# Feed-forward stage of an encoder trunk: joining copies ordered behind the last weight cast, and every weight unit cast in two pieces

## The chip, the cores and the metric

The kernel runs on one core of a Trainium2 chip. The metric is the device time of one execution in microseconds. TensorE (PE) does the matrix products and loads its weights beside them (PEld), VectorE (DVE), ScalarE (ACT) and GpSimd (POOL) do the rest, and SyncE (SP) issues the DMAs.

## The reference

Two layers of an encoder block on 256 tokens of width 1024, in float32. Each layer mixes a gated linear attention and a grouped-query attention, and is followed by a SwiGLU feed-forward stage of hidden width 2816, which is where the change acts, and by a per-layer embedding:

```python
gate, up = jnp.split(rms_norm(h, g_ffn_pre) @ w_ffn_in, 2, axis=-1)
h = h + rms_norm((jax.nn.silu(gate) * up) @ w_ffn_out, g_ffn_post)
e = p_i @ w_ple_proj
h = h + rms_norm(jax.nn.sigmoid(h @ w_ple_gate) * e, g_ple_post)
```

## The kernel before

**Products in three parts.** Every float32 operand of a product is split into a high part (a rounding to the format fp32r) and a low part, the remainder. A product is three matmuls: high by high, high by low, low by high (`mm3`, line 98). `split` (line 110) makes the parts: a cast on ScalarE (line 112) and a subtraction on VectorE (line 108).

**The stream of weights.** All weights come through `Stream` (line 210) in units of 128 x 2048, 1 MB each. A unit is loaded by SP into one of two buffers `raw` (line 259), is cast into a tile `wh` on ScalarE, and its remainder goes into `wl` on VectorE. The pools hold four `wh` and four `wl` tiles, so that a cast waits until TensorE has read the unit that held its slot. `take` hands the next unit to TensorE's code, `done` returns one, and `fill` then writes the casts of further units into the program, up to `depth` units ahead. `put` (line 265) cuts the unit into `parts` pieces, each with its own cast and subtraction: two halves of 128 x 1024, or the whole of 128 x 2048 while `ws.wide` is set.

**The feed-forward stage.** The hidden width is cut into 11 blocks of 256. The string `FFN` (line 38) gives the order in which the stage works through units: `u` is one of two units of a plain block (`block`, line 1268; 24 matmuls of 128x512), `1` to `7` are the seven steps of a pair of blocks (`pair`, `seven`; 12 matmuls each), `o` is a unit of the output matrix for both halves of the tokens (24 matmuls). The pair follows a scheme with seven products instead of eight, for which sums of weight units are made on VectorE (line 289). For these, two units are loaded into tiles lent from the `wh` and `wl` pools (in the profile `lent`), one into a tile `big`, and the fourth comes later as `raw`. Steps 3 to 5 and 7 of a pair add to the accumulator of an earlier step in place; before step 7 that accumulator must have been read by the subtraction that follows step 5 (`times(a, form(3), False, lambda: vsub(p5, p5, a))`, line 630).

**The transposes of the hidden values.** The gated values of a block lie with tokens on the partitions; the output product needs them transposed. `turn_words` (line 391) does this by DMA, with a generator in three stages: ScalarE copies the 16-bit words apart (line 401); SP issues the transposing DMA (line 407); ScalarE joins the words (line 413 for a plain block, line 419 for a half of a pair's), and `Split.put` casts the result and subtracts (tiles `big`, lines 112 and 108). Between the stages it yields a number of ticks, and a tick follows every few matmuls in the program's text. With `far` set, which is so for the feed-forward stage's blocks outside the last pair, the buffers of the last two stages are two halves of one tile `mid`.

**What sets the order.** A scheduler orders each engine's instructions by its own estimate of when they can run; each engine then works strictly in that order. `tc.issue_after(ins)` ties the instructions that a block traces on the engine of `ins` behind `ins`.

Of the kernel before, what the change touches and what calls it, by code (L numbers as in the profile page):

```python
# [18 lines left out]
P = 128  # L19
T = 256  # L20
# [30 lines left out]
def trunk_kernel(ctx: ExitStack, tc: tile.TileContext, a: dict, out: bass.AP):  # L51
# [7 lines left out]
    nc = tc.nc  # L59
# [13 lines left out]
    def nm(s):  # L73
        uid[0] += 1
        return f"{s}_{part[0]}_{uid[0]}"

    def big(dt=F32):
        return bigp.tile([P, 2048], dt, tag="big", name=nm("big"))

    def mid(dt=F32):  # L80
        return b4p.tile([P, 1024], dt, tag="mid", name=nm("mid"))
# [7 lines left out]
    def t512():  # L89
        return smp.tile([P, 512], F32, tag="t512", name=nm("t512"), bufs=7)  # L90
# [16 lines left out]
    def vsub(out, in0, in1):  # L107
        nc.vector.tensor_tensor(out=out, in0=in0, in1=in1, op=ALU.subtract)  # L108

    def split(hi, lo, src):  # L110

        nc.scalar.copy(hi, src)  # L112
        vsub(lo, src, hi.bitcast(F32))


    h = cp.tile([P, 2, D], F32, tag="h", name="h")
# [21 lines left out]
    def unit(w, kh, c0):  # L138

        return lambda t: [  # L140
            (
                t[:, :2048].rearrange("p (k c) -> p k c", c=512),
                w[kh * 512 : (kh + 1) * 512, c0 : c0 + 512].rearrange("(k p) c -> p k c", p=P),
            )
        ]
# [28 lines left out]
    for l in range(DEPTH):  # L174
# [12 lines left out]
        pairs = [[unit(w, kh, c + b * 256) for kh in range(2) for c in (0, HIDDEN)] for b in PAIRS]  # L187
# [9 lines left out]
    class Load:  # L197


        def __init__(self, make, own=None, waits=False):  # L200
            self.make, self.own, self.waits, self.raw, self.n = make, own, waits, None, 0
# [8 lines left out]
    class Stream:  # L210
# [7 lines left out]

        def __init__(self, depth):
            self.depth, self.held, self.room, self.ready, self.open = depth, 0, 0, [], False  # L220
            self.loads, self.jobs, self.lend, self.wide = [], [], False, False
            pairs = {}
            for item in plan:
                if callable(item):
                    x = Load(item)
                    self.loads.append(x)
                    self.jobs.append(lambda x=x: self.plain(x))
                else:
                    units, n = item
                    if n == 1:  # L230
                        b11, b12, b21, b22 = units
                        x, z = (Load(b, lambda tag=tag: self.lent(tag), tag == "wh") for b, tag in ((b11, "wh"), (b12, "wl")))
                        y, q = Load(b22, big), Load(b21)
                        pairs[id(units)] = x, y, z, q
                        self.loads += [x, y, z]
                    if n == 5:
                        self.loads.append(q)
                    self.jobs.append(lambda p=pairs[id(units)], n=n: self.step(n, *p))
# [23 lines left out]
                    between()  # L262
                x.n = sum(math.prod(dst.shape[1:]) for dst, _ in moves)

        def put(self, x, parts=None):

            wh = wp.tile([P, UNIT], F32R, tag="wh", name=nm("wh"))
            wl = wp.tile([P, UNIT], F32R, tag="wl", name=nm("wl"))
            self.ready.append((wh, wl))
            self.held += 1  # L270
            parts = parts or (1 if self.wide else 2)
            cuts = [slice(j * x.n // parts, (j + 1) * x.n // parts) for j in range(parts)]
            return [(wh[:, c], wl[:, c], x.raw[:, c]) for c in cuts]

# [6 lines left out]

        def made(self, x):
            for piece in self.put(x):
                split(*piece)

        def step(self, n, x, y, z, q):
            def add(to, other):
# [18 lines left out]
        def fill(self):  # L306
            while self.open and self.held < self.depth and self.jobs:
                pieces = self.jobs.pop(0)()
                for piece in pieces or ():
                    split(*piece)  # L310
                if pieces:
                    self.load()

# [9 lines left out]
    ws = Stream(4)  # L323
# [36 lines left out]
    class Split:  # L360
# [30 lines left out]
        def turn_words(self, src, k, n, hf=None, far=False):  # L391

            x = lambda: t512()[:, : n * P * (2 if hf is None else 1)]
            w = x()
            w16 = w.bitcast(U16)  # L400
            nc.scalar.copy(
                w16.rearrange("p (s c) -> p s c", s=2), src.bitcast(U16).rearrange("p (c s) -> p s c", s=2)
            )
            yield SENT
            r, z = [t[:, : n * P * (2 if hf is None else 1)] for t in halves(mid())] if far else (x(), None)
            r16 = r.bitcast(U16)
            nc.sync.dma_start_transpose(out=r16.rearrange("p (r t) -> p r t", t=P), in_=w16)
            yield LANDED
            z = x() if z is None else z
            z16 = z.bitcast(U16)  # L410
            if hf is None:
                for i in range(2):
                    nc.scalar.copy(
                        z16.rearrange("p (k h t s) -> p h s k t", k=2, h=2, s=2)[:, i],
                        r16.rearrange("p (s h k t) -> p h s k t", h=2, k=2, s=2)[:, i],
                    )
                self.put(z, k, n, 0, T)
            else:
                nc.scalar.copy(z16.rearrange("p (c s) -> p s c", s=2), r16.rearrange("p (s c) -> p s c", s=2))
                self.put(z, k, n, hf * P, P)  # L420

        def tok(self, k, hf):
            return [t[:, 0, :] for t in self.at(k, 1, hf * P, P)]
# [68 lines left out]
    def halves(t):  # L492
        return [t[:, j * 512 : (j + 1) * 512] for j in range(2)]
# [309 lines left out]
    for l in range(DEPTH):  # L803
# [219 lines left out]
        for x in range(2):  # L1023
            o = project_t(uT)
            for i in range(2):
                dst = qk[:, x, 2 * i : 2 * i + 2, :]
                src = o[i].rearrange("p (h t) -> p h t", t=T)
# [165 lines left out]
        for br in range(2):  # L1193
            t = big().rearrange("p (s c) -> p s c", s=2)
# [129 lines left out]
        steps, pairs, seven_ = chain.from_iterable(block(b) for b in PLAIN), list(PAIRS), None  # L1324
        for x in FFN:
            if x == "p":
                gpost = gain(a["g_ffn_post"][l], mid(), D)
                pin = mid()[:, 0:512].rearrange("p (s c) -> p s c", c=256)
                nc.sync.dma_start(pin, a["p"][l, 0].rearrange("(s p) c -> p s c", p=P))
                pT = [t.rearrange("p (k t) -> p k t", t=T) for t in halves(mid(F32R))]  # L1330
                embedded = Task(turn_p_in(), f"{l}emb")
                continue
            if x == "o":
                n, w = outs.pop(0), ws.take()
                for hf in range(2):
                    out_step(n, hf, w)
                ws.done()
                continue
            if x == "1":
                seven_ = pair(pairs.pop(0))  # L1340
            next(steps if x == "u" else seven_)
            ws.wide = x in "234567" and len(pairs) > 0 or ws.wide and x != "3"
        ws.lend = False

        if l + 1 < DEPTH:
# [21 lines left out]
        for hf in range(2):  # L1367
            s = slice(hf * P, (hf + 1) * P)
# [85 lines left out]
```

## Time and profile before

| | us |
|---|---|
| three runs | 934.84, 933.96, 930.89 |
| their median | 933.96 |
| the profiled execution | 932.07 |
| its span, first to last instruction | 930.4 |
| TensorE busy in the span | 911.5 |
| VectorE, ScalarE busy | 721.4, 622.8 |
| feed-forward stage of layer 0, layer 1 | 281.7 to 439.0, 737.5 to 895.0 |
| granted clock of TensorE | 0.997 |

A row of the timeline gives start, duration, engine, line, operation, written tile <- read tiles, shape and count; in brackets stands the idle time of the engine before it, and what ended it. The number in a tile's name (0ffnin) is the layer and the part of the program. Matmuls overlap: one lasts 0.39 us, and the next starts 0.23 us after its start when nothing is missing, so a gap from start to start above 0.23 us is time lost, also where the row shows no idle time. Line numbers are those of the kernel before.

### The profile page before, as it was taken

How to read it: one execution, taken by the hardware profiler on the slowest of the kernel's cores; microseconds unless marked ns; L12 is line 12 of the kernel's file. 1: busy time of each engine (PE TensorE's matmuls, PEld its weight loads, DVE VectorE, ACT ScalarE, POOL GpSimd, SP SyncE). 2: the span in 40 equal slices, each digit the busy share in tenths (PEclk: the TensorE clock that was granted, in tenths of full speed). 3: DMA queues.
4: the chain of work that ended last, by engine and by line, in shares of the span. 5: the costliest groups of instructions: out<-in, count | busy, mean ns of one | idle time of the engine just before them, and what ended most of it. 6: DMA issues, size and time to landing. Idle time of an engine off the chain costs nothing.

```text
span 930.4 us, 12115 instructions
## 1 busy us (share of the span) xinstructions
PE 911.5 (98%) x4577; PEld 770.7 (83%) x4577; DVE 721.4 (78%) x871; ACT 622.8 (67%) x952; POOL 84.6 (9%) x150
## 2 busy tenths in 40 slices
PE   9999999999999989999999999999999998999996
PEld 7998888888878777888899988888888787788786
DVE  5798977656569798898689789665566797989874
ACT  5569678735477776667765686785545876857663
POOL 3500211100000000000123002100001000000000
PEclk9999999999999999999999999999999999999998
DMA  7464456857376665846555525396664856765551
GB/s 250 150 227 135 138 180 179 290 188 211 97 250 212 204 217 185 276 145 239 174 182 181 182 91 161 123 273 214 205 213 143 271 174 203 238 232 174 181 181 46
DMA packets 119896, 177.11 MB, mean 190 GB/s; under 512 B 35159, under 2 KB 58199, under 8 KB 119838
## 3 DMA queue, kind: packets, MB, share of 16 engines
q1 hardware_dynamic: 119838, 176.34, 59.1%
q8 instruction: 36, 0.59, 0.3%
q14 instruction: 22, 0.18, 0.1%
HBM read 167.41 MB, written 1.05 MB: 181 GB/s over the span
## 4 chain that ended last, share of the span: by engine, by line
PE 82%; ACT 5%; DMA 4%; DVE 4%; issue 3%; POOL 2%; SPq 0%; POOLq 0%; DVEq 0%; ACTq 0%
PE acc_1ffnin L96 10%; PE acc_0ffnin L96 9%; PE acc_1ffnin L573 5%; PE acc_1gate L96 5%; PE acc_0gate L96 5%; PE acc_1merge L96 5%; PE acc_0merge L96 5%; PE acc_0ffnin L573 4%; PE acc_1gqk L96 2%; PE acc_0gqk L96 2%; PE acc_0rq L96 2%; PE acc_1ple L96 2%; PE acc_0gg L96 2%; PE acc_1gg L96 2%; PE acc_1v L96 2%
## 5 line engine op out<-in xcount | busy, mean ns | idle before, releaser
L96 PE MATMUL acc_1ffnin<-wh_1ffnin,big_1ffnin 128*128 128x512 f32 x176 | 56.6, 392 | 0.0
L96 PE MATMUL acc_0ffnin<-wh_0ffnin,big_0ffnin 128*128 128x512 f32 x176 | 56.1, 391 | 0.0
L108 DVE TENSOR_TENSOR wl_1ffnin<-raw_1ffnin,wh_1ffnin 128x1024 fp32r<-128x1024 f32 (+1 forms) x26 | 43.9, 1713 | 6.5 <-ACT wh_1ffnin L112 6.4
L108 DVE TENSOR_TENSOR wl_0ffnin<-raw_0ffnin,wh_0ffnin 128x1024 fp32r<-128x1024 f32 (+1 forms) x26 | 43.8, 1713 | 6.0 <-ACT wh_0ffnin L112 5.6
L112 ACT CAST wh_0ffnin<-raw_0ffnin 128x1024 fp32r<-128x1024 f32 (+1 forms) x26 | 36.8, 1450 | 16.7 <-DMA raw_0ffnin<-in_w_ffn_out_dram 14.1
L112 ACT CAST wh_1ffnin<-raw_1ffnin 128x1024 fp32r<-128x1024 f32 (+1 forms) x26 | 37.0, 1447 | 16.1 <-DMA raw_1ffnin<-in_w_ffn_out_dram 6.9
L108 DVE TENSOR_TENSOR wl_0ffnin<-lent_0ffnin,wh_0ffnin 128x2048 fp32r<-128x2048 f32 (+1 forms) x19 | 34.6, 1839 | 7.9 <-ACT wh_0ffnin L112 7.9
L108 DVE TENSOR_TENSOR wl_1ffnin<-lent_1ffnin,wh_1ffnin 128x2048 fp32r<-128x2048 f32 (+1 forms) x19 | 34.6, 1838 | 7.8 <-ACT wh_1ffnin L112 7.8
L96 PEld LDWEIGHTS acc_1ffnin<-wh_1ffnin,big_1ffnin 128*128 128x128 f32 x176 | 33.0, 188 | 7.1 <-ACT big_1ffnin L112 0.2
L96 PEld LDWEIGHTS acc_0ffnin<-wh_0ffnin,big_0ffnin 128*128 128x128 f32 x176 | 33.0, 188 | 7.1 <-ACT big_0ffnin L112 0.3
L112 ACT CAST wh_0ffnin<-lent_0ffnin 128x2048 fp32r<-128x2048 f32 (+1 forms) x19 | 29.2, 1551 | 8.1 <-DVE lent_0ffnin L289 3.3
L96 PE MATMUL acc_1ffnin<-wl_1ffnin,big_1ffnin 128*128 128x512 f32 x88 | 34.3, 390 | 0.0
L96 PE MATMUL acc_0ffnin<-wl_0ffnin,big_0ffnin 128*128 128x512 f32 x88 | 34.2, 390 | 0.0
L112 ACT CAST wh_1ffnin<-lent_1ffnin 128x2048 fp32r<-128x2048 f32 (+1 forms) x19 | 29.1, 1549 | 7.5 <-DVE lent_1ffnin L289 3.1
L573 PE MATMUL acc_0ffnin<-wh_0ffnin,mid_0ffnin 128*128 128x512 f32 x96 | 31.3, 392 | 0.6 <-ACT wh_0ffnin L112 0.6
L573 PE MATMUL acc_1ffnin<-wh_1ffnin,mid_1ffnin 128*128 128x512 f32 x96 | 31.3, 392 | 0.5 <-ACT wh_1ffnin L112 0.5
L96 PE MATMUL acc_0ffnin<-wh_0ffnin,big_0wout 128*128 128x512 f32 x96 | 30.4, 390 | 0.0
L96 PE MATMUL acc_1ffnin<-wh_1ffnin,big_1wout 128*128 128x512 f32 x96 | 30.4, 389 | 0.0
L108 DVE TENSOR_TENSOR wl_1gate<-raw_1gate,wh_1gate 128x1024 fp32r<-128x1024 f32 x14 | 16.5, 1222 | 15.2 <-ACT wh_1gate L112 15.2
L108 DVE TENSOR_TENSOR wl_0gate<-raw_0gate,wh_0gate 128x1024 fp32r<-128x1024 f32 x14 | 17.2, 1273 | 11.8 <-ACT wh_0gate L112 11.7
L573 PE MATMUL acc_1ffnin<-wh_1ffnin,big_1wout 128*128 128x512 f32 x72 | 23.5, 392 | 2.5 <-DVE mid_1ffnin L108 2.5
L573 PE MATMUL acc_0ffnin<-wh_0ffnin,big_0wout 128*128 128x512 f32 x72 | 23.5, 392 | 2.4 <-DVE mid_0ffnin L108 2.3
(659 smaller groups left out, 2970.2 us busy)
## 6 DMA issues: line engine op xcount, KB each, us to landing
raw_0ffnin<-in_w_ffn_out_dram SPq DMA_DIRECT2D x11, 1024.0 KB, 5.6
raw_1ffnin<-in_w_ffn_out_dram SPq DMA_DIRECT2D x11, 1024.0 KB, 4.9
lent_0ffnin<-in_w_ffn_in_dram SPq DMA_DIRECT2D x6, 1024.0 KB, 7.4
lent_1ffnin<-in_w_ffn_in_dram SPq DMA_DIRECT2D x6, 1024.0 KB, 5.8
raw_0rq<-in_w_in_dram SPq DMA_DIRECT2D x4, 1024.0 KB
raw_0v<-in_w_in_dram SPq DMA_DIRECT2D x4, 1024.0 KB
raw_0gg<-in_w_in_dram SPq DMA_DIRECT2D x4, 1024.0 KB, 5.0
raw_0gate<-in_w_o_gla_dram SPq DMA_DIRECT2D x4, 1024.0 KB, 5.3
```

The costliest lines, as they stand in the source:

```text
L96: return nc.tensor.matmul(o, lhsT, rhs, start=start, stop=stop)
L108: nc.vector.tensor_tensor(out=out, in0=in0, in1=in1, op=ALU.subtract)
L112: nc.scalar.copy(hi, src)
L573: nc.tensor.matmul(o, x, y, start=first and k + n == 0, stop=k == 3 and n == 2, skip_group_check=not first)
```

## The change

Two edits. `split` returns its cast, and `Stream` keeps the cast of the weight piece that was traced last in `ws.cast`. In `turn_words` with `far`, the joining copies and the casts of `put` behind them are tied behind that cast. And `ws.wide` is dropped, so that `put` always makes two pieces.

```diff
     def split(hi, lo, src):
 
-        nc.scalar.copy(hi, src)
+        cast = nc.scalar.copy(hi, src)
         vsub(lo, src, hi.bitcast(F32))
+        return cast
...
-        def put(self, x, parts=None):
+        def put(self, x, parts=2):
...
-            parts = parts or (1 if self.wide else 2)
...
         def made(self, x):
             for piece in self.put(x):
-                split(*piece)
+                self.cast = split(*piece)
...
                 for piece in pieces or ():
-                    split(*piece)
+                    self.cast = split(*piece)
...
             z16 = z.bitcast(U16)
-            if hf is None:
-                for i in range(2):
-                    nc.scalar.copy(
...
-                self.put(z, k, n, 0, T)
-            else:
...
+            with tc.issue_after(ws.cast.ins) if far else nullcontext():
+                if hf is None:
+                    for i in range(2):
+                        nc.scalar.copy(
...
+                    self.put(z, k, n, 0, T)
+                else:
...
-            ws.wide = x in "234567" and len(pairs) > 0 or ws.wide and x != "3"
```

Where `ws.wide` was set, from step 2 of the first pair to step 2 of the last, 25 units of each layer were cast whole; they are now cast in halves. Names below carry the tile's number, which is the same in both programs, and then a count of instructions, which is not; lines from 113 on stand one lower in the program of the change.

ScalarE in layer 0, from a cast for step 5 of the first pair on (`wh_445`, `wh_448`, `wh_454` serve steps 5, 6 and 7, `wh_456` a plain block, `wh_463` the first unit of the output matrix; `mid_447` is what the DMA has transposed). Before:

```order
L112 CAST wh_0ffnin_445_2911<-lent_0ffnin_393_2593 128x2048
L401 COPY t512_0ffnin_444_2896<-t512_0ffnin_432_2798 128x1024
L112 CAST wh_0ffnin_448_2931<-raw_0ffnin_431_2796 128x2048
L413 COPY mid_0ffnin_447_2922<-mid_0ffnin_447_2922 128x2x2x128 x2
L112 CAST wh_0ffnin_454_2964<-lent_0ffnin_391_2589 128x2048
L112 CAST big_0ffnin_440_2882<-mid_0ffnin_447_2922 128x2x256
L112 CAST wh_0ffnin_456_2968<-raw_0ffnin_443_2889 128x2048
L112 CAST wh_0ffnin_463_3011<-raw_0ffnin_453_2962 128x2048
```

and with the change:

```order
L112 CAST wh_0ffnin_445_2913<-lent_0ffnin_393_2593 128x1024 x2
L401 COPY t512_0ffnin_444_2898<-t512_0ffnin_432_2798 128x1024
L112 CAST wh_0ffnin_448_2935<-raw_0ffnin_431_2796 128x1024 x2
L112 CAST wh_0ffnin_454_2970<-lent_0ffnin_391_2589 128x1024 x2
L112 CAST wh_0ffnin_456_2976<-raw_0ffnin_443_2891 128x1024 x2
L414 COPY mid_0ffnin_447_2926<-mid_0ffnin_447_2926 128x2x2x128 x2
L112 CAST wh_0ffnin_463_3021<-raw_0ffnin_453_2968 128x1024
L112 CAST big_0ffnin_440_2882<-mid_0ffnin_447_2926 128x2x256
L112 CAST wh_0ffnin_463_3021<-raw_0ffnin_453_2968 128x1024
```

The joining copies have moved behind the casts for step 7 and for the plain block, and the cast of their result stands between the halves of the unit after that.

VectorE in layer 0, around the second pair (`wl_483` and `wl_496` are units of the output matrix, `wl_491` and `wl_493` steps 3 and 4; `big_489` and `big_494` are transposed hidden values; rows of line 289 are sums of weight units, the last with the late fourth unit `raw_484`). Before:

```order
L108 TENSOR_TENSOR wl_0ffnin_483_3114<-raw_0ffnin_461_2978,wh_0ffnin_482_3113 128x2048
L289 TENSOR_TENSOR lent_0ffnin_458_2972<-lent_0ffnin_458_2972,big_0ffnin_459_2974 128x2048
L108 TENSOR_TENSOR big_0ffnin_489_3136<-mid_0ffnin_472_3050,big_0ffnin_489_3136 128x4x128
L108 TENSOR_TENSOR big_0ffnin_489_3136<-mid_0ffnin_473_3064,big_0ffnin_489_3136 128x4x128
L108 TENSOR_TENSOR wl_0ffnin_491_3141<-lent_0ffnin_458_2972,wh_0ffnin_490_3140 128x2048
L108 TENSOR_TENSOR wl_0ffnin_493_3161<-big_0ffnin_459_2974,wh_0ffnin_492_3160 128x2048
L108 TENSOR_TENSOR big_0ffnin_494_3191<-mid_0ffnin_481_3105,big_0ffnin_494_3191 128x2x256
L108 TENSOR_TENSOR wl_0ffnin_496_3195<-raw_0ffnin_465_3015,wh_0ffnin_495_3194 128x2048
L289 TENSOR_TENSOR lent_0ffnin_458_2972<-lent_0ffnin_458_2972,raw_0ffnin_484_3117 128x2048
```

and with the change:

```order
L108 TENSOR_TENSOR wl_0ffnin_483_3130<-raw_0ffnin_461_2988,wh_0ffnin_482_3129 128x1024
L289 TENSOR_TENSOR lent_0ffnin_458_2982<-lent_0ffnin_458_2982,big_0ffnin_459_2984 128x2048
L108 TENSOR_TENSOR wl_0ffnin_483_3130<-raw_0ffnin_461_2988,wh_0ffnin_482_3129 128x1024
L108 TENSOR_TENSOR big_0ffnin_489_3154<-mid_0ffnin_472_3064,big_0ffnin_489_3154 128x4x128
L108 TENSOR_TENSOR wl_0ffnin_491_3159<-lent_0ffnin_458_2982,wh_0ffnin_490_3158 128x1024 x2
L108 TENSOR_TENSOR big_0ffnin_489_3154<-mid_0ffnin_473_3078,big_0ffnin_489_3154 128x4x128
L108 TENSOR_TENSOR wl_0ffnin_493_3181<-big_0ffnin_459_2984,wh_0ffnin_492_3180 128x1024 x2
L289 TENSOR_TENSOR lent_0ffnin_458_2982<-lent_0ffnin_458_2982,raw_0ffnin_484_3135 128x2048
L108 TENSOR_TENSOR big_0ffnin_494_3213<-mid_0ffnin_481_3121,big_0ffnin_494_3213 128x2x256
L108 TENSOR_TENSOR wl_0ffnin_496_3217<-raw_0ffnin_465_3027,wh_0ffnin_495_3216 128x1024 x2
```

The second subtraction of `big_489` has moved behind step 3's remainder, and the sum that reads `raw_484` has moved ahead of the remainder `wl_496`.

TensorE in layer 0, at the end of the second pair's step 5 (`wh_500` is a unit of the output matrix, `wh_503` serves step 6). Before:

```order
L573 MATMUL acc_0ffnin_487_3121<-wh_0ffnin_498_3213,mid_0ffnin_417_2698 128x512
L96 MATMUL acc_0ffnin_477_3083<-wh_0ffnin_500_3231,big_0ffnin_489_3136 128x512
L96 MATMUL acc_0ffnin_478_3084<-wh_0ffnin_500_3231,big_0ffnin_489_3136 128x512
L96 MATMUL acc_0ffnin_479_3085<-wh_0ffnin_500_3231,big_0ffnin_489_3136 128x512
L96 MATMUL acc_0ffnin_480_3086<-wh_0ffnin_500_3231,big_0ffnin_489_3136 128x512
L573 MATMUL acc_0ffnin_514_3320<-wh_0ffnin_503_3261,big_0wout_366_2427 128x512
L96 MATMUL acc_0ffnin_477_3083<-wl_0ffnin_501_3232,big_0ffnin_489_3136 128x512
```

and with the change:

```order
L574 MATMUL acc_0ffnin_487_3139<-wh_0ffnin_498_3237,mid_0ffnin_417_2698 128x512
L96 MATMUL acc_0ffnin_477_3099<-wh_0ffnin_500_3257,big_0ffnin_489_3154 128x512
L96 MATMUL acc_0ffnin_478_3100<-wh_0ffnin_500_3257,big_0ffnin_489_3154 128x512
L96 MATMUL acc_0ffnin_479_3101<-wh_0ffnin_500_3257,big_0ffnin_489_3154 128x512
L96 MATMUL acc_0ffnin_477_3099<-wl_0ffnin_501_3258,big_0ffnin_489_3154 128x512
```

Where TensorE did five matmuls of this and the next unit ahead of the first that reads the remainder `wl_501`, it now does three.

More of the change, by code (lines that the diff above doesn't have):

```diff
@@ L220, in __init__ @@
             self.depth, self.held, self.room, self.ready, self.open = depth, 0, 0, [], False
-            self.loads, self.jobs, self.lend, self.wide = [], [], False, False
+            self.loads, self.jobs, self.lend = [], [], False
             pairs = {}
@@ L410, in turn_words @@
             z16 = z.bitcast(U16)
-            if hf is None:
-                for i in range(2):
[L413 to L416, printed above, removed]
-                self.put(z, k, n, 0, T)
-            else:
-                nc.scalar.copy(z16.rearrange("p (c s) -> p s c", s=2), r16.rearrange("p (s c) -> p s c", s=2))
-                self.put(z, k, n, hf * P, P)
+            with tc.issue_after(ws.cast.ins) if far else nullcontext():
+                if hf is None:
+                    for i in range(2):
+                        nc.scalar.copy(
+                            z16.rearrange("p (k h t s) -> p h s k t", k=2, h=2, s=2)[:, i],
+                            r16.rearrange("p (s h k t) -> p h s k t", h=2, k=2, s=2)[:, i],
+                        )
+                    self.put(z, k, n, 0, T)
+                else:
+                    nc.scalar.copy(z16.rearrange("p (c s) -> p s c", s=2), r16.rearrange("p (s c) -> p s c", s=2))
+                    self.put(z, k, n, hf * P, P)
         def tok(self, k, hf):
```

## The prediction

> **What bounds the kernel now.** I read the page, then TensorE's waits, then the feed-forward stage as a stretch, then the timeline around each hole.
>
> ```profile
> span 930.4 us, 12115 instructions
> PE 911.5 (98%) x4577; PEld 770.7 (83%) x4577; DVE 721.4 (78%) x871; ACT 622.8 (67%) x952; POOL 84.6 (9%) x150
> ```
>
> TensorE is busy for 911.5 of 930.4 us, so a change of order can win only its holes, some 19 us over the program. Its list of waits (total, times, longest) names those of the feed-forward stage:
>
> ```profile
> PE acc_1ffnin L573 <- DVE mid_1ffnin L108: 2.5, 1, 2.5
> PE acc_0ffnin L573 <- DVE mid_0ffnin L108: 2.3, 1, 2.3
> ...
> PE acc_0ffnin L573 <- ACT wh_0ffnin L112: 0.6, 1, 0.6
> PE acc_1ffnin L573 <- ACT wh_1ffnin L112: 0.5, 1, 0.5
> ```
>
> One long and one short hole in each layer. The stretch of layer 0's stage (length, then busy time of TensorE, its weight loads, VectorE, ScalarE, GpSimd, granted clock, DMA share, GB/s) shows who could hold TensorE up:
>
> ```profile
> 281.70:439.00 157.30, 154.19 (x681) 125.24 (x680) 140.37 (x110) 111.59 (x117) 1.83 (x3) 1.00 0.64 207
> ```
>
> VectorE works 140.37 of 157.30 us, 89%; ScalarE has room. Now the long hole in the timeline, with ScalarE, VectorE and TensorE around it:
>
> ```profile
> 314.82 0.39 PE L96 MATMUL acc_0ffnin<-wh_0ffnin,big_0wout 128*128 128x512 f32 x1
> 315.38 0.50 PE L96 MATMUL acc_0ffnin<-wl_0ffnin,big_0wout 128*128 128x512 f32 x1 [0.17 <-DVE wl_0ffnin L108]
> ...
> 316.64 1.92 ACT L112 CAST wh_0ffnin<-raw_0ffnin 128x2048 fp32r<-128x2048 f32 x1
> 322.43 1.40 ACT L413 COPY mid_0ffnin<-mid_0ffnin 128x512 uint16<-128x512 uint16 x2 [3.87 <-DMA mid_0ffnin<-t_0ffnin]
> 323.70 1.90 ACT L112 CAST wh_0ffnin<-lent_0ffnin 128x2048 fp32r<-128x2048 f32 x1
> 325.63 2.29 DVE L108 TENSOR_TENSOR wl_0ffnin<-lent_0ffnin,wh_0ffnin 128x2048 fp32r<-128x2048 f32 x1 [4.74 <-ACT wh_0ffnin L112]
> 327.84 0.68 DVE L108 TENSOR_TENSOR mid_0ffnin<-mid_0ffnin,acc_0ffnin 128x512 f32<-128x512 f32 x1
> ...
> 325.93 0.39 PE L573 MATMUL acc_0ffnin<-wh_0ffnin,big_0wout 128*128 128x512 f32 x1
> 328.66 0.47 PE L573 MATMUL acc_0ffnin<-wh_0ffnin,big_0wout 128*128 128x512 f32 x1 [2.34 <-DVE mid_0ffnin L108]
> ```
>
> It is a chain. ScalarE stands 3.87 us before the joining copies, whose transposing DMA has not landed; the weight cast of 323.70 is queued behind them; VectorE stands 4.74 us for that cast; behind its remainder stands the short subtraction of 327.84, which frees the accumulator that TensorE's last step of the pair needs. Layer 1 has the same:
>
> ```profile
> 781.04 0.39 PE L573 MATMUL acc_1ffnin<-wh_1ffnin,big_1wout 128*128 128x512 f32 x1
> 783.90 0.47 PE L573 MATMUL acc_1ffnin<-wh_1ffnin,big_1wout 128*128 128x512 f32 x1 [2.47 <-DVE mid_1ffnin L108]
> ```
>
> **The change, part by part.** Half a percent is 4.7 us here, about what a measurement of this kernel can tell from no change. The sum needs TensorE's pace and the other holes:
>
> ```profile
> 353.49 0.39 PE L573 MATMUL acc_0ffnin<-wh_0ffnin,mid_0ffnin 128*128 128x512 f32 x1
> 354.43 0.50 PE L573 MATMUL acc_0ffnin<-wh_0ffnin,mid_0ffnin 128*128 128x512 f32 x1 [0.56 <-ACT wh_0ffnin L112]
> 354.96 0.50 PE L573 MATMUL acc_0ffnin<-wl_0ffnin,mid_0ffnin 128*128 128x512 f32 x1
> ...
> 406.74 0.61 PE L573 MATMUL acc_0ffnin<-wh_0ffnin,mid_0ffnin 128*128 128x512 f32 x2
> 407.19 1.07 PE L96 MATMUL acc_0ffnin<-wh_0ffnin,big_0ffnin 128*128 128x512 f32 x4
> 408.27 0.49 PE L573 MATMUL acc_0ffnin<-wh_0ffnin,big_0wout 128*128 128x512 f32 x1
> 408.64 0.50 PE L573 MATMUL acc_0ffnin<-wl_0ffnin,mid_0ffnin 128*128 128x512 f32 x1
> ```
>
> Two matmuls from 406.74 to 407.19: 0.23 us from start to start. What goes beyond that is a hole: A, the long one, 2.73 - 0.23 = 2.50 in layer 0 and 2.86 - 0.23 = 2.63 in layer 1. B, at 353.49, 1.47 - 0.46 = 1.0, and by the 0.5 against 0.6 of the waits 0.9 in layer 1. C, at 314.82, 0.56 - 0.23 = 0.3, layer 0 only. D, at 407.19, 1.45 - 5 x 0.23 = 0.3, and I take 0.2 for layer 1. Together 7.8 us.
>
> Cost of the split, from pairs of halves and whole units:
>
> ```profile
> 306.53 2.01 ACT L112 CAST wh_0ffnin<-big_0ffnin 128x1024 fp32r<-128x1024 f32 x2
> 312.78 1.92 ACT L112 CAST wh_0ffnin<-lent_0ffnin 128x2048 fp32r<-128x2048 f32 x1
> ...
> 307.62 2.36 DVE L108 TENSOR_TENSOR wl_0ffnin<-big_0ffnin,wh_0ffnin 128x1024 fp32r<-128x1024 f32 x2 [0.28 <-ACT wh_0ffnin L112]
> 318.59 2.29 DVE L108 TENSOR_TENSOR wl_0ffnin<-raw_0ffnin,wh_0ffnin 128x2048 fp32r<-128x2048 f32 x1
> ```
>
> Two halves cost ScalarE 0.09 and VectorE 0.07 us more. With 25 whole units in a layer (12 raw, 11 lent, 2 big) that is 2.2 and 1.8 us a layer. ScalarE has 45 us of room; for VectorE it is 1.8 of 17 free, hidden unless VectorE sets the pace (below). In return VectorE may begin 0.9 us earlier, and TensorE once half a remainder is ready, 1.1 us earlier.
>
> Hole A. The cast behind the copies waits only for its slot, which TensorE frees at the end of the block unit begun at 314.82: 24 matmuls and hole C later, about 320.8. So the cast runs from 320.9, the remainders' halves from 322.0 to 324.3, the subtraction to 325.0. TensorE wants it at 325.8 (C being gone). No wait, with 0.8 us to spare: all of A goes.
>
> The copies themselves now run two casts later, near 325, when their DMA has long landed. Queued behind them on ScalarE is the next cast, whose slot TensorE frees only at 325.9 (the step that begins the hole in the rows above), so that it loses about half a microsecond of a lead of several. TensorE needs the copies' tile only in a later block of the output matrix: the second pair's copies are subtracted by 350.3, and TensorE reads that tile after 356. I cost that at nothing; were this cover gone, each copy would cost what it is late. Their DMAs are issued ahead of them and stay in SP's order.
>
> What is late next is VectorE, as from 322.0 it has no idle time to lose. Up to the first half of the remainder that follows the next pair's fourth step it has 8 units at 2.28 (pairs, start to start), 4 sums at 2.21, 8 short ones at 0.60, 0.7 for the two gate products and a half at 1.1: 33.6 us, so 355.6. A pair of copies (1.40 us in the row above) now stands between two casts that VectorE follows closely, so I add 1.4 us of waits for ScalarE, an estimate: 357.0. TensorE wanted this at 353.49 + 24 x 0.23 + 1.0 + 0.2, about 360.2; without A, B and C 356.4. B goes, since its first half is ready by 348.2 (the same chain as far as that unit) for a step that begins at 353.49 - 2.8 = 350.7. But a new wait of 0.6 us appears. One load later comes another. Its rows:
>
> ```profile
> 347.60 0.37 SPq L259 DMA_DIRECT2D raw_0ffnin<-in_w_ffn_in_dram  x1
> 359.94 12.00 SPq L259 DMA_DIRECT2D raw_0ffnin<-in_w_ffn_out_dram  x3
> ...
> 359.83 2.28 DVE L289 TENSOR_TENSOR lent_0ffnin<-lent_0ffnin,raw_0ffnin 128x2048 f32<-128x2048 f32 x1
> 365.11 3.72 ACT L112 CAST wh_0ffnin<-raw_0ffnin 128x2048 fp32r<-128x2048 f32 x2 [4.87 <-DMA raw_0ffnin<-in_w_ffn_out_dram]
> ```
>
> The load issued at 359.94, when the remainder before it had freed the buffer, is cast at 365.11, 5.2 us later. With the change it is issued at 358.2, cast at 363.4, and half its remainder is ready at 365.5; TensorE comes at 365.1. Wait 0.4. In the last pair the same working leaves spare times between 0 and 0.5 us, and D goes; I add nothing. So 1.0 us per layer is given back, 2.0 in all.
>
> Two more moves. In layer 0 a cast and a subtraction for layer 1's decay weights move between the two halves of a norm, at most 1.2 us on its chain. After the norm's last step
>
> ```profile
> 433.53 1.42 DVE L530 SCALAR_TENSOR_TENSOR h<-mid_0ffnout,rstd_0ffnout,h 128x512 f32<-128x512 f32 x2 [0.36 <-POOL rstd_0ffnout L486]
> 437.80 1.08 ACT L112 CAST big_0ffnout<-aux_0ffnout 128x512 fp32r<-128x512 f32 x2 [1.18 <-PE aux_0ffnout L432]
> ```
>
> at 434.95 TensorE's transposes follow only some 2 us later, so this is hidden. On SP a small load moves behind one weight load, which costs nothing as its reader is 16 ticks away.
>
> The sum: 7.8 - 2.0 = 5.8 us. The profiled execution took 932.07 us, 1.7 more than its span, and becomes 926.3. It was 1.9 us below the median of the three runs, 933.96; against that the forecast is 928.2.
>
> **The rivals.** First, the gain is given back at the moved sums. In two pairs per layer the sum of line 289 that reads a freshly loaded unit moves on VectorE ahead of the remainder TensorE wants next. It now ran at 359.83, 12 us after its load was issued. With the change the load goes out when six of the eight units, three sums, five short ones and the gate products are done, 24.0 us and 0.4 of waiting after 322.0, so at 346.4. The sum stands at the head of the queue at 357.0 less a half (1.1), a short one (0.6) and itself (2.2), so at 353.1, 6.7 us later. The loads on the profile's page land after
>
> ```profile
> raw_0ffnin<-in_w_ffn_out_dram SPq DMA_DIRECT2D x11, 1024.0 KB, 5.6
> ...
> lent_0ffnin<-in_w_ffn_in_dram SPq DMA_DIRECT2D x6, 1024.0 KB, 7.4
> ```
>
> At 5.6 us it is in time; at 7.4 VectorE stands 0.7 us at each of four places. 5.8 - 2.8 = 3.0 us of gain, 931.0: no change by the half percent. I choose 5.6, since this load goes out first of its burst.
>
> Second, slower: VectorE sets the pace and TensorE loses its filling. Now, at 407.19 and 408.27, TensorE does five matmuls of later units while a remainder is missing; the new order has none there, and at the second pair three instead of five. If the halves come no earlier than the wholes now, seven matmuls follow the waits, 7 x 0.23 = 1.6 us a layer, and the split's 1.8 us comes into the open: 2 x 3.4 = 6.8 us, 940.8. It decides if the half remainder I put at 357.0 comes after 360.2. For it speaks VectorE at 89%, against it that the 4.74 us of idle time go just before. [...]
>
> Third, the copies move but something unseen holds the cast of 323.70: 933.96, no change.
>
> **How the numbers follow.** Forecast 0.61, first rival 0.30, second 0.07, third 0.02. The range runs from all 7.8 us won on the profiled execution, 924.3, to the first rival's 931.0 plus the 0.9 by which the highest of the three runs, 934.84, exceeds the median, 931.9. Faster by over half a percent 0.62 (the forecast, and a little of the first rival), within it 0.31, slower 0.07.
>
> **What would show it.** Right: no ScalarE wait of 3.9 us before line 414's copies, no TensorE wait on the subtraction, VectorE idle under 1 us there; then TensorE waits of 0.4 to 0.8 us on VectorE's remainders a pair later. The first rival shows as VectorE waits for a load before line 289. Wrong altogether: A remains, or waits of TensorE on remainders add up to more than 5 us a layer.

## The result and the profile after

| | before | after |
|---|---|---|
| median (lowest to highest), us | 934.31 (930.89 to 934.84, 4 runs) | 924.15 (923.10 to 924.65, 4 runs) |
| profiled execution, us | 932.07 | 924.19 |

The ratio is 0.9902, 95% interval 0.9883 to 0.9921: about 1% faster, where 0.6% was forecast. The time lies 0.15 us below the low end of the range in microseconds; as a ratio to the runs beside it, 0.9902, it is just inside (924.3 of 933.96 is 0.9897). In a second comparison (e0 below) it was 924.00 against 932.59, 0.9915 [0.9902, 0.9929].

The head of the page of after, the span and each engine's busy time:

```profile
span 922.5 us, 12213 instructions
PE 909.2 (99%) x4577; PEld 771.5 (84%) x4577; DVE 724.3 (79%) x921; ACT 626.1 (68%) x1002; POOL 82.6 (9%) x150
```

TensorE does the same 4577 matmuls. Its list of waits (total, times, longest), from the third entry:

```profile
PE aux_0ple L433 <- DVE mid_0ple L491: 0.8, 2, 0.5
PE aux_0ffnin L433 <- DVE t_0ffnin L105: 0.7, 1, 0.7
PE acc_1rq L96 <- DVE wl_0ple L108: 0.4, 1, 0.4
PE acc_0ffnin L96 <- DVE wl_0wout L108: 0.4, 2, 0.2
```

The waits on `mid_0ffnin` and `mid_1ffnin`, 2.3 and 2.5 us, are gone, and so are the ones on `wh_0ffnin` and `wh_1ffnin`. One is new in the stage: 0.7 us on a gate product of the last pair. The stretch in which VectorE was 140.37 us busy now reads

```profile
281.70:439.00 157.30, 156.49 (x699) 128.57 (x698) 145.54 (x141) 118.45 (x152) 3.64 (x4) 1.00 0.66 215
```

VectorE is 145.54 of 157.30 us busy (93%), partly since the next stage now begins inside the stretch; from 282.0 to 435.2, the stage alone, it is 141.6 of 153.2. TensorE misses 0.8 us. The chain of the long hole, in the timeline of after:

```profile
320.42 2.00 ACT L112 CAST wh_0ffnin<-lent_0ffnin 128x1024 fp32r<-128x1024 f32 x2 [2.24 <-PE acc_0ffnin L96]
321.50 2.36 DVE L108 TENSOR_TENSOR wl_0ffnin<-lent_0ffnin,wh_0ffnin 128x1024 fp32r<-128x1024 f32 x2 [1.18 <-ACT wh_0ffnin L112]
323.78 0.68 DVE L108 TENSOR_TENSOR mid_0ffnin<-mid_0ffnin,acc_0ffnin 128x512 f32<-128x512 f32 x1
324.99 1.40 ACT L414 COPY mid_0ffnin<-mid_0ffnin 128x512 uint16<-128x512 uint16 x2
325.38 0.61 PE L574 MATMUL acc_0ffnin<-wh_0ffnin,big_0wout 128*128 128x512 f32 x2
325.83 0.39 PE L574 MATMUL acc_0ffnin<-wl_0ffnin,big_0wout 128*128 128x512 f32 x1
```

The cast no longer stands behind a DMA; what it waits for is its slot, which TensorE frees (2.24 us, on `acc_0ffnin`). VectorE's idle time before the remainder fell from 4.74 to 1.18 us, the short subtraction ends at 324.46, and TensorE goes from 325.38 to 325.83 without a break. The copies come at 324.99, and no wait of TensorE names them.

How much each stage gave shows in the first and last starts of its matmuls (min, median and longest ns, then first and last start). Before, in layer 0:

```profile
L96 PE MATMUL acc_0ffnin<-wh_0ffnin,big_0wout x96: 387/389/402, 281.9 to 336.7; 128*128 128x512 f32 x96
L96 PE MATMUL acc_0ffnin<-wh_0ffnin,big_0ffnin x176: 387/389/501, 336.9 to 439.2; 128*128 128x512 f32 x176
```

After:

```profile
L96 PE MATMUL acc_0ffnin<-wh_0ffnin,big_0wout x96: 389/389/389, 282.1 to 333.5; 128*128 128x512 f32 x96
L96 PE MATMUL acc_0ffnin<-wh_0ffnin,big_0ffnin x176: 387/389/476, 333.8 to 435.3; 128*128 128x512 f32 x176
```

From 281.9 to 439.2 it took 157.3 us, from 282.1 to 435.3 it takes 153.2: 4.1 us less. Layer 1 by the same rows: 737.7 to 894.1, then 733.9 to 886.2, also 4.1. Together that is 8.2 us; the span is 7.9 us shorter, so that the rest of the program differs by 0.3 the other way.

### The profile page after: what moved, and what is told of

It reads as the page before. It is cut to its first block, busy times and chain, and to the rows that moved or that the text cites. A ratio compares the mean times of both kernels' runs of the same rounds, so it can differ in the third digit from the quotient of the medians.

```text
span 922.5 us, 12213 instructions
## 1 busy us (share of the span) xinstructions
PE 909.2 (99%) x4577; PEld 771.5 (84%) x4577; DVE 724.3 (79%) x921; ACT 626.1 (68%) x1002; POOL 82.6 (9%) x150
## 3 DMA queue, kind: packets, MB, share of 16 engines
HBM read 167.41 MB, written 1.05 MB: 183 GB/s over the span
## 4 chain that ended last, share of the span: by engine, by line
PE 75%; DVE 10%; DMA 6%; ACT 4%; issue 3%; POOL 2%; SPq 0%; POOLq 0%; ACTq 0%; DVEq 0%
PE acc_1ffnin L96 10%; PE acc_0ffnin L96 6%; PE acc_1gate L96 5%; PE acc_0gate L96 5%; PE acc_1merge L96 5%; PE acc_0merge L96 5%; PE acc_1ffnin L574 4%; DVE wl_0ffnin L108 3%; PE acc_1gqk L96 2%; PE acc_0rq L96 2%; PE acc_0gqk L96 2%; DMA raw_0ffnin<-in_w_ffn_out_dram 2%; PE acc_1ple L96 2%; PE acc_1gg L96 2%; PE acc_0gg L96 2%
## 5 line engine op out<-in xcount | busy, mean ns | idle before, releaser
L108 DVE TENSOR_TENSOR wl_1ffnin<-raw_1ffnin,wh_1ffnin 128x1024 fp32r<-128x1024 f32 x38 | 45.0, 1218 | 6.4 <-ACT wh_1ffnin L112 6.4
L112 ACT CAST wh_0ffnin<-raw_0ffnin 128x1024 fp32r<-128x1024 f32 x38 | 38.3, 1050 | 17.1 <-DMA raw_0ffnin<-in_w_ffn_out_dram 14.6
L112 ACT CAST wh_1ffnin<-raw_1ffnin 128x1024 fp32r<-128x1024 f32 x38 | 38.4, 1048 | 17.0 <-DMA raw_1ffnin<-in_w_ffn_out_dram 8.9
L108 DVE TENSOR_TENSOR wl_0ffnin<-raw_0ffnin,wh_0ffnin 128x1024 fp32r<-128x1024 f32 x38 | 44.9, 1219 | 6.1 <-ACT wh_0ffnin L112 6.1
L112 ACT CAST wh_0ffnin<-lent_0ffnin 128x1024 fp32r<-128x1024 f32 x30 | 30.2, 1050 | 10.2 <-DVE lent_0ffnin L289 4.0
L108 DVE TENSOR_TENSOR wl_0ffnin<-lent_0ffnin,wh_0ffnin 128x1024 fp32r<-128x1024 f32 x30 | 35.3, 1218 | 1.6 <-ACT wh_0ffnin L112 1.6
L112 ACT CAST wh_1ffnin<-lent_1ffnin 128x1024 fp32r<-128x1024 f32 x30 | 30.2, 1050 | 8.9 <-PE acc_1ffnin L96 3.5
L108 DVE TENSOR_TENSOR wl_1ffnin<-lent_1ffnin,wh_1ffnin 128x1024 fp32r<-128x1024 f32 x30 | 35.3, 1217 | 1.2 <-ACT wh_1ffnin L112 1.2
L96 PE MATMUL acc_0rq<-wh_start,big_start 128*128 128x384 f32 (+1 forms) x96 | 25.4, 349 | 0.9 <-ACT big_start L123 0.9
L96 PE MATMUL acc_1gate<-wh_1gate,big_0ple 128*128 128x512 f32 x80 | 24.8, 389 | 0.0
```

What stands on the lines that cost most here:

```text
L96: return nc.tensor.matmul(o, lhsT, rhs, start=start, stop=stop)
L112: cast = nc.scalar.copy(hi, src)
```

## Experiments

All ratios are against runs of the kernel before on the same chip. Theory at the start: the tie removes the long hole and the split only shortens what follows. Rival: the split does most of it, since first halves come early, and the tie little.

**e0, the changed kernel again**, without an edit.

> The changed kernel once more, as the yardstick for the three beside it. Its first timing was 0.990 of before; its two traces differ by 7.9 us, while the holes that I counted and that are gone sum to 8.8 us in the two feed-forward stages. If the stages are all there is to it, the ratio is 0.990 to 0.992.

924.00 us, 0.9915 [0.9902, 0.9929], as expected.

**e1, the tie alone.** Against the changed kernel:

```
-        def put(self, x, parts=2):
+        def put(self, x, parts=None):
...
+            parts = parts or (1 if self.wide else 2)
```

> Only the tie of the joining copies; units are cast whole where they were before. Theory (the copies' place in ScalarE's queue opens the long hole, A): A is gone in both layers, 5.1 us and the restarts, while TensorE waits up to 1.1 us longer at each place where it now waits for the first half of a remainder, some two places a layer: 0.993 to 0.996 of before. Rival (the split alone does it, since a half remainder frees TensorE 1.1 us earlier): A stays or shrinks by 1.1 us at most, 0.998 to 1.000.

936.07 us, 1.0045 [1.0029, 1.0061]: slower, which neither side had. The long hole is gone in both layers, yet the time isn't. TensorE's order, as built, at the third step of the second pair (unit 492's high and low words are `wh_0ffnin_492` and `wl_0ffnin_493`):

```
L575 MATMUL acc_0ffnin_488_3122<-wh_0ffnin_492_3160,mid_0ffnin_409_2674 128x512
L96 MATMUL acc_0ffnin_477_3083<-wh_0ffnin_495_3194,big_0ffnin_489_3136 128x512
L96 MATMUL acc_0ffnin_478_3084<-wh_0ffnin_495_3194,big_0ffnin_489_3136 128x512
L96 MATMUL acc_0ffnin_479_3085<-wh_0ffnin_495_3194,big_0ffnin_489_3136 128x512
L96 MATMUL acc_0ffnin_480_3086<-wh_0ffnin_495_3194,big_0ffnin_489_3136 128x512
L575 MATMUL acc_0ffnin_488_3122<-wl_0ffnin_493_3161,mid_0ffnin_409_2674 128x512
```

Four matmuls of unit 495 stand ahead of unit 492's last eleven. In the changed kernel all of 492's come first. The timeline of e1 at that place:

```profile
352.01 1.90 ACT L112 CAST wh_0ffnin<-raw_0ffnin 128x2048 fp32r<-128x2048 f32 x1
352.08 0.61 PE L575 MATMUL acc_0ffnin<-wh_0ffnin,mid_0ffnin 128*128 128x512 f32 x2
...
353.95 0.74 PE L96 MATMUL acc_0ffnin<-wh_0ffnin,big_0ffnin 128*128 128x512 f32 x2 [1.26 <-ACT wh_0ffnin L112]
```

TensorE waits 1.26 us for unit 495's whole cast, with 492's matmuls behind it. New theory: with whole units the tie loses what it won, partly by this order and partly because whole remainders come late.

**e2, the split alone** (no `issue_after` in `turn_words`, halves as in the changed kernel).

```
-            with tc.issue_after(ws.cast.ins) if far else nullcontext():
+            with nullcontext():
```

> Only the split; the joining copies stay where they were before. Theory: ScalarE stands again some 3.9 us before the copies of the first pair's plain block and TensorE's wait on the subtraction stays, at 2.5 us less at most 1.1 for the earlier half: 1.5 to 2.5 us a layer. C and part of B go. 0.996 to 0.999 of before. Rival (the split alone does it): no wait on the subtraction, 0.990 to 0.992.

929.94 us, 0.9971 [0.9961, 0.9981]. The long hole stays (2.4 and 1.5 us), the short ones on casts go. One of 1.1 us in layer 0 and one of 0.5 in layer 1 come, both on a gate product of the last pair. So the tie alone is +0.45%, the split alone -0.3%, and both together -0.85% to -1.0%: the joint effect is not the sum of the two, which would be +0.15%.

**e4, the tie and four pieces.**

```
-            parts = parts or (1 if self.wide else 2)
+            parts = parts or (4 if self.wide else 2)
```

> The change, but four pieces of 128x512 instead of two where before had one. VectorE has 11.6 us idle in the changed kernel's stage; 50 more pieces a layer at 0.07 us cost it 3.5 us, ScalarE 4.5 us. Theory (VectorE's time lies beside TensorE except at single places where a first half is awaited): 0 to 1.5 us a layer longer, 0.990 to 0.994 of before. Rival (VectorE is saturated and sets the pace): 3.5 us a layer longer, 0.997 to 0.999.

922.81 us, 0.9898 [0.9883, 0.9913]. Cutting each unit twice as often costs nothing that shows. It is the fastest kernel tried, but its interval overlaps the changed kernel's: a gain over it isn't shown.

**e5, whole cast, subtraction in two** (with the tie).

```
+        cast = nc.scalar.copy(hi, src)
+        m = src.shape[-1] // 2
+        for c in (slice(0, m), slice(m, 2 * m)):
+            vsub(lo[:, c], src[:, c], hi[:, c].bitcast(F32))
```

> The tie, the cast of a unit whole and only its subtraction in two. The tie alone cost 0.45%. Theory: it lost because whole remainders come late and because TensorE's order put four matmuls of unit 495 ahead of unit 492's last eleven, so that they waited 1.3 us for unit 495's cast. Here the remainders are halved, and 492's matmuls stand together ahead of 495's: nearly the whole gain comes back, 0.990 to 0.994. Rival, that the half casts carry the gain (a first half after 1.05 us instead of a whole cast of 1.91): the waits on casts stay, 0.998 to 1.003.

928.66 us, 0.9949 [0.9934, 0.9965]: 0.96% better than the tie alone, but not the whole. What is left is a wait on a whole cast, in TensorE's list of e5:

```profile
PE acc_0ffnin L96 <- ACT wh_0ffnin L118: 1.0, 1, 1.0
...
PE acc_1ffnin L96 <- ACT wh_1ffnin L118: 0.8, 1, 0.8
```

In layer 0 it lasts from 364.2 to 365.2, and the whole cast that ends it began at 363.23, when its load had landed. The first half of a cast takes 1.05 us (the mean in the changed kernel) instead of 1.91 (the mean in the kernel before), so that by this estimate TensorE would have had it at 364.3. At this place the half cast counts too.

**e6, cast in two, whole subtraction** (with the tie).

```
+        for c in (slice(0, m), slice(m, 2 * m)):
+            cast = nc.scalar.copy(hi[:, c], src[:, c])
+        vsub(lo, src, hi.bitcast(F32))
```

> The tie, the cast of a unit in two and its subtraction whole. Unit 495's four matmuls stand ahead of unit 492's last eleven, as with the tie alone. Theory (late remainders and that order): the loss stays, 0.999 to 1.005, with waits of about 1 us on whole remainders near 366 and 404 us of layer 0. Rival (the half casts carry the gain): 0.990 to 0.995.

936.89 us, 1.0035 [1.0020, 1.0050], in the range of the theory. Its order still has unit 495 ahead of 492. At the head of its list stands, in each layer, a wait on a whole remainder, in layer 0 at 368.6:

```profile
PE acc_0ffnin L96 <- DVE wl_0ffnin L108: 1.9, 1, 1.9
PE acc_1ffnin L96 <- DVE wl_1ffnin L108: 1.8, 1, 1.8
```

The other place that the theory names, near 404, has a wait too, of 1.2 us at 405.1, but on a copy of ScalarE.

**e7, whole units, only the whole blocks' copies tied.**

```
-            with tc.issue_after(ws.cast.ins) if far else nullcontext():
+            with tc.issue_after(ws.cast.ins) if far and hf is None else nullcontext():
```

> Whole units as before, and only the joining copies of whole blocks (two copies of 128x512) stand behind the cast; those of the pairs' halves are where they were before. Theory: the long hole goes in both layers (2.5 and 2.6 us), unit 492's matmuls stand together, and the waits on whole units further on stay as in the kernel before: 0.994 to 0.997. Rival (any tie with whole units only moves the wait to the next pair): 1.000 to 1.006.

930.57 us, 0.9974 [0.9961, 0.9987], between the two ranges: the long hole goes, but waits of 0.6 and 1.0 us on whole remainders come at 357.8 and 367.7 of layer 0 (1.6 us in all, 1.5 in layer 1). Against e1, which differs from it by the tie of the pairs' copies alone, it is 0.7% faster: with whole units it is the pairs' tie that makes e1 lose, and unit 495 no longer stands ahead of 492.

**e8, the tie and eight pieces.**

```
-            parts = parts or (1 if self.wide else 2)
+            parts = parts or (8 if self.wide else 2)
```

> The tie and eight pieces of 128x256 where the kernel before had a whole unit. Four pieces made VectorE 145.5 us busy in the 153.2 us from 282.0 to 435.2, 3.9 more than two pieces, or 0.08 us for each of 50 cuts. Theory: 100 more cuts add about 8 us, VectorE is saturated at 153 of 153 us, and sets the pace in places: 0.991 to 1.000. By the rival of the prediction, that a saturated VectorE takes TensorE's filling, 1.003 to 1.012. If pieces cost nothing even here: 0.988 to 0.991.

932.59 us, 0.9988 [0.9975, 1.0002]. The gain of e4 is gone again. Eight subtractions of 128x256, one behind the other, take 2.76 us in this trace, four of 128x512 in e4's 2.49, where a whole one took 2.29. TensorE's list of e8 has waits on remainders again:

```profile
PE acc_0ffnin L96 <- DVE wl_0ffnin L108: 2.2, 3, 1.1
PE acc_1ffnin L96 <- DVE wl_1ffnin L108: 1.7, 2, 1.1
```

The first half of the second rival's mechanism, that VectorE sets the pace, appears here in places, two doublings further on than the change goes: from 387 to 417 of layer 0 VectorE has no idle time, and two of the three waits lie there (at 393.7 and 408.5). But two of the three, 1.1 us at 345.9 and 0.5 at 393.7, come where a sum of 2.28 us stands on VectorE between the first eighth and the second. One matmul of the stage reads 512 columns (128x512 in its rows) and an eighth has 256, so that an eighth alone frees none. How much of the loss is VectorE's work, how much its order, and how much the changed order of TensorE (which again puts a matmul of unit 549 ahead of the last twenty of unit 546), no run here separates. Nor do the waits hold all of the loss: 2.1 us come in the per-layer embedding right behind layer 0's stage.

The busy share alone doesn't tell the good case from the bad one: of the 153.2 us from 282.0 to 435.2 VectorE is busy for 141.6 with two pieces, 145.5 with four and 146.9 with eight.

**e9, the tie with whole units, TensorE's order by units.** Every matmul of a step is placed behind the last one of the step before:

```
+    def behind_unit(f, *args, **kw):
+        with tc.issue_after(unit_end[0].ins) if unit_end[0] is not None else nullcontext():
+            unit_end[1] = f(*args, **kw)
...
+            unit_end[0] = unit_end[1]
             if x == "o":
```

> The tie with whole units, and TensorE's matmuls of one unit of the FFN's steps all behind the last one of the unit traced before, which is the order by units that the changed kernel has. The tie alone gave 1.0045 with 8.0 and 8.4 us of TensorE's time lost in the two FFN stages. Theory A (the order is half of that loss, whole remainders the other half): the waits near 352 us of layer 0 and 809 of layer 1 (1.3 and 1.4 us) go, those near 366, 403, 822 and 860 stay: 1.000 to 1.003. Theory B (the order is nearly all of it): 0.992 to 0.996. Theory C (late remainders are all of it, and the order only shows them): 1.004 to 1.008.

931.26 us, 0.9981 [0.9971, 0.9991], between theories A and B. The order of its units is that of the changed kernel, except that in layer 1 two units of the output matrix change places near the end. Taken first, the order is worth 0.64% (1.0045 to 0.9981), and the halves then another 0.66% (to e0's 0.9915); the halves with the old order were not run. With the order mended, the whole remainder itself is what TensorE waits for (timeline of e9):

```profile
353.47 2.28 DVE L115 TENSOR_TENSOR wl_0ffnin<-big_0ffnin,wh_0ffnin 128x2048 fp32r<-128x2048 f32 x1
...
355.81 0.50 PE L99 MATMUL acc_0ffnin<-wl_0ffnin,mid_0ffnin 128*128 128x512 f32 x1 [2.11 <-DVE wl_0ffnin L115]
```

A half would have been there some 1.1 us earlier, by the 2.28 us of a whole subtraction and 1.22 of a half (an estimate).

**e10, halves, only the whole blocks' copies tied** (the edit of e7 in the changed kernel).

```
-            with tc.issue_after(ws.cast.ins) if far else nullcontext():
+            with tc.issue_after(ws.cast.ins) if far and hf is None else nullcontext():
```

> The changed kernel with the tie on the joining copies of whole blocks alone; those of the pairs' halves aren't tied. TensorE's order is that of the split alone (0.9971). Theory: the tie of the whole blocks' copies carries what the tie adds to the split, the long holes of 2.4 and 1.5 us: 0.991 to 0.994. Rival (the pairs' copies carry half of it): 0.994 to 0.997.

924.20 us, 0.9903 [0.9885, 0.9920]. TensorE's order here is that of e2 matmul for matmul, so the step from 0.9971 to 0.9903 is the tie's alone, and all of it that shows comes from the whole blocks' copies.

**e11, halves, only the pairs' copies tied.**

```
-            with tc.issue_after(ws.cast.ins) if far else nullcontext():
+            with tc.issue_after(ws.cast.ins) if far and hf is not None else nullcontext():
```

> The changed kernel with the tie on the joining copies of the pairs' halves alone; those of whole blocks aren't tied. Theory: the long hole stays in both layers, and the time is that of the split alone or somewhat more: 0.996 to 1.000. Rival (the pairs' copies carry half of the gain): 0.992 to 0.995.

928.80 us, 0.9958 [0.9945, 0.9972], just beside the low end of the expectation; its interval overlaps that of the split alone. The long hole stays with 0.7 us in layer 0 and 1.8 in layer 1.

**e12, whole units, no tie, TensorE's order by units** (against e9).

```
-            with tc.issue_after(ws.cast.ins) if far else nullcontext():
+            with nullcontext():
```

> The kernel before with whole units and no tie, and TensorE's matmuls of one unit all behind those of the unit traced before. With the tie, this order was worth 0.64% (1.0045 to 0.9981). Theory: without the tie the old order hurts little, since its hoisted matmuls fill holes while a copy stands ahead of the cast; the long hole stays: 0.998 to 1.003. Rival, that the split's gain by itself (0.9971) was the order that it brings: 0.996 to 0.998.

934.85 us, 1.0011 [0.9999, 1.0023]. The order of e9 (but for three matmuls a layer), worth 0.64% behind the tie, is worth nothing without it: the long hole is 3.0 and 2.5 us here, since the matmuls that filled a part of it are gone, and in its profile both holes are followed by a stretch at half the clock (0.52 from 329.20 to 332.60, 0.55 from 786.40 to 790.20; last section), an estimated 1.6 us each. With whole units, then, the order by itself does not give what the split gives.

## Why the prediction was right, and where its sizes were off

**The long hole: right, to half a microsecond.** Cast forecast at 320.9, seen at 320.42; remainders 322.0 to 324.3, seen 321.50 to 323.86; end of the subtraction 325.0, seen 324.46. The copies came at the forecast 325, and cost nothing. That the whole blocks' copies are the ones that count is shown by e10 and e11. Of the signs listed, ScalarE's wait before the copies and TensorE's on the subtraction are gone as forecast; VectorE's idle time is 1.18 us and not under 1, since the half cast that it follows takes 1.0 to 1.1 us. With hole A the third rival fell.

**What was listed as holes: too little.** Adding up what every distance from the start of a 128x512 matmul to the next start has above 0.23 us gives 5.7 us in layer 0 (281 to 441) and 4.9 in layer 1 (733 to 896) before, 1.8 and 0.9 after. That is 7.9 us won, net of what is given back, and just what the two profiles differ by. With the 1.6 us given back (next paragraph) 9.5 us of holes went, where the list had four places with 7.8 us. It left out that the matmul after the first one of a restart is late too, by about 0.1 us each time (0.31 to 0.34 us from start to start in before at 315.71, 328.97, 355.30 and 784.21, where 0.23 is the pace), and four smaller breaks in layer 0 (at 303.7, 345.1, 369.4 and 425.2, together 0.9). So the term was 1.7 us too small.

**What is given back: near in sum, wrong in make-up.** Forecast 2.0 us, by two waits in each layer; found 1.6. The first came where it was expected, in the timeline of after:

```profile
354.78 2.35 DVE L108 TENSOR_TENSOR wl_0ffnin<-raw_0ffnin,wh_0ffnin 128x1024 fp32r<-128x1024 f32 x2
...
355.52 0.39 PE L96 MATMUL acc_0ffnin<-wh_0ffnin,big_0ffnin 128*128 128x512 f32 x1
356.05 0.50 PE L96 MATMUL acc_0ffnin<-wl_0ffnin,big_0ffnin 128*128 128x512 f32 x1
```

0.53 - 0.23 = 0.3, and 0.1 for the next matmul: 0.4 instead of 0.6, and 0.4 in layer 1 too (at 807.4). VectorE's chain was counted as 33.6 us from 322.0, plus 1.4 for waits on ScalarE, to 357.0; the half remainder was ready at about 356.0. The chain began 0.5 us earlier, at 321.50, and took 34.5, 0.9 more than counted; VectorE's waits for ScalarE in it are two of 0.3 us (before 348.75 and 349.70), so that the 1.4 was too much. As the half remainder came 1.0 us early, the second wait fell away:

```profile
357.16 0.37 SPq L260 DMA_DIRECT2D raw_0ffnin<-in_w_ffn_out_dram  x1
...
362.21 3.90 ACT L112 CAST wh_0ffnin<-raw_0ffnin 128x1024 fp32r<-128x1024 f32 x4 [5.53 <-DMA raw_0ffnin<-in_w_ffn_out_dram]
363.30 4.63 DVE L108 TENSOR_TENSOR wl_0ffnin<-raw_0ffnin,wh_0ffnin 128x1024 fp32r<-128x1024 f32 x4 [3.29 <-ACT wh_0ffnin L112]
364.12 0.84 PE L96 MATMUL acc_0ffnin<-wh_0ffnin,big_0ffnin 128*128 128x512 f32 x3
364.80 0.39 PE L96 MATMUL acc_0ffnin<-wl_0ffnin,big_0ffnin 128*128 128x512 f32 x1
```

The load goes out 1.0 us earlier than forecast, half its remainder is ready at 364.5, and TensorE wants its next one at 364.80: no wait where 0.4 stood. In its place came one that no step of the prediction has, at the end of layer 0's stage:

```profile
417.99 0.39 PE L96 MATMUL acc_0ffnin<-wl_0ffnin,big_0ffnin 128*128 128x512 f32 x1
418.22 1.29 DVE L105 TENSOR_TENSOR t_0ffnin<-mid_0ffnin,t_0ffnin 128x512 f32<-128x512 f32 x2
419.05 0.63 PE L433 MATMUL aux_0ffnin<-ident,t_0ffnin 128*128 128x128 f32 x4 [0.68 <-DVE t_0ffnin L105]
```

Four transposes that read a gate product of the last pair now stand in TensorE's order where VectorE has not yet made it; before, all eight stood together, later in the order, and waited for nothing. 1.06 - 0.23 = 0.8 us. The runs e2, e4 and e10 have this wait too (1.1, 0.8 and 0.9 us), those with whole units don't. Together 0.4 + 0.4 + 0.8 = 1.6 us.

**The first rival fell.** The moved sum with a fresh load runs without idle time before it:

```profile
351.98 2.28 DVE L289 TENSOR_TENSOR lent_0ffnin<-lent_0ffnin,raw_0ffnin 128x2048 f32<-128x2048 f32 x1
```

So do the other three, at 396.5, 803.8 and 847.4.

**The second rival fell at two pieces, and its price for the filling was wrong.** It counted seven matmuls moved out of the holes as 2 x 1.6 us lost. e12 puts the order by units at 1 us without the tie (0.11%, interval from -0.01% to 0.23%), and e1 against e9 at 6 us in the other direction with it. A matmul placed ahead fills a hole only when its own operand is there before the hole ends: in e1 the four of unit 495 waited 1.26 us for their own cast.

**What the sum did not show.** It names the earlier halves (0.9 and 1.1 us) and builds on them in its holes A and B, but it never asks what the tie would do with whole units, and it takes the order of TensorE as something that may cost. The experiments give half of what parts tie and changed kernel to that order, when it is mended first, and the other half to the halves. Priced alone, the tie would have been forecast as faster (the expectation of e1 says so), and it is slower. That the order comes out otherwise because the scheduler reckons with the length of whole pieces is likely, but was only argued.

**From profile to median.** The forecast moved from the profiled execution to the median by a fixed 1.9 us. The two comparisons differ by 10.2 and 8.6 us where the profiles differ by 7.9. So of the 4.4 us by which 10.2 exceeds the forecast 5.8, 1.7 are holes that were not listed, 0.4 what was given back less, and 2.3 lie between profile and median. The forecast took that step as the same before and after; that the difference there went the way of the forecast is luck. In the 29 runs of the kernel before that stand beside e5 to e8, those with a mean granted clock of 0.997 took 929.6 us on the mean (3 runs), 0.996 932.3 (17), 0.995 934.3 (5), 0.994 934.5 (3), and one at 0.993 935.1. After, the clock is 0.997 to 0.999 in all nine runs, and they lie within 1.6 us. Part of this may be the stretch at half the clock that the last section describes: it takes some 1.6 us, and 0.002 of the mean clock (3.4 us at 0.50 in 930), and before's profile has none in its two stages (1.00 in both). By its clock a common run of before, at 0.996, has one (an estimate: behind the last matmul the clock is 0.50 too, in before from 926.0 to 930.4, and the profiles whose stages have no such stretch are at 0.997 to 0.999, so that 0.996 needs one more). The steps from clock to clock are larger than this gives, and their rest stays open.

## What to carry to other kernels

When a queue is reordered to remove a wait, follow the next two consumers with the sizes that their pieces will really have: here the reordering was worth 0.6 to 0.7% with halves and cost 0.45% with wholes. Two edits of one chain should be tried alone and together before either is credited or thrown out, and the instruction order of the waiting engine compared each time, as it can change without being edited. Cut work into smaller pieces while the engine has room for what each cut costs (about 0.07 us on VectorE here), and no finer than the reader takes it: here four pieces of 512 columns, what one matmul reads, were as good as two, and eight lost the gain.

## What the hardware showed that was not expected

**After five of ten waits of 1.8 to 3.0 us TensorE ran at half the clock for some 3.4 us.** Stretches of e9 (length, busy times of TensorE, weight loads, VectorE, ScalarE, GpSimd, granted clock, DMA share, GB/s) after the 2.1-us waits in layer 0 and in layer 1:

```profile
356.30:359.50 3.20, 3.20 (x9) 2.46 (x8) 3.20 (x3) 1.42 (x1) 0.00 (x0) 0.50 0.00 0
...
811.80:815.20 3.40, 3.40 (x17) 2.79 (x16) 3.40 (x3) 1.44 (x1) 0.00 (x0) 1.00 0.04 7
```

In the first the clock is 0.50 and nine matmuls run in 3.2 us, in the second 1.00 and seventeen in 3.4. Around the first, from 356.00 to 359.60, the mean clock is 0.53, and from 359.60 on it is 1.00, so that the stretch lasts some 3.4 us. The same in e2 behind its 2.4-us wait and in e11 behind 1.8 us:

```profile
329.20:332.70 3.50, 3.50 (x10) 2.69 (x9) 3.50 (x6) 1.84 (x3) 0.00 (x0) 0.51 0.98 367
```

```profile
782.40:785.50 3.10, 3.10 (x8) 2.35 (x8) 3.10 (x4) 2.32 (x3) 0.00 (x0) 0.50 1.03 392
```

Seventeen matmuls in 3.4 us would be sixteen in 3.2: seven are missing in the stretch of e9, at 0.23 us each 1.6 us (an estimate). Among the profiles of this study there are ten waits of 1.8 to 3.0 us in the two stages:

| run, layer | wait, us | granted clock behind it |
|---|---|---|
| e12, 0 | 3.0 | 0.52 (329.20 to 332.60) |
| e12, 1 | 2.5 | 0.55 (786.40 to 790.20) |
| before, 1 | 2.5 | 1.00 (784.10 to 787.60) |
| e2, 0 | 2.4 | 0.51 (329.20 to 332.70) |
| before, 0 | 2.3 | 1.00 (328.90 to 332.40) |
| e9, 0 | 2.1 | 0.50 (356.30 to 359.50) |
| e9, 1 | 2.1 | 1.00 (811.80 to 815.20) |
| e6, 0 | 1.9 | 1.00 (the stage's mean) |
| e6, 1 | 1.8 | 1.00 (the stage's mean) |
| e11, 1 | 1.8 | 0.50 (782.40 to 785.50) |

The stages with the stretches of e2, e9 and e11 have a mean clock of 0.99; the other stages of these three, and both of before, after, e1, e4 to e8 and e10, are at 1.00. The length of the wait alone doesn't tell which are followed: 2.5 us in before were not, 1.8 us in e11 were, and the 2.1 us of e9 were in one layer and not in the other. What decides it was not shown.

**On VectorE a cut cost half of what the durations say.** The subtraction took 2.29 us whole (before), 2 x 1.22 in halves (after), 4 x 0.685 in quarters (e4) and 8 x 0.414 in eighths (e8): about 0.15 us for each further cut. Pieces that run one behind the other take 2.36 us for two, 2.49 for four and 2.76 for eight: 0.07 us for a cut, since the end of one overlaps the start of the next (by 0.08 us in after, where the pair of 321.50 ends at 323.86 and the next instruction starts at 323.78).
